# Attention outputs by blocks of keys, 512 queries wide, in two output and two transposition banks

## The chip, the cores and the metric

The kernel runs on one core of a Trainium2 chip. The core has TensorE (PE, with its weight loads as PEld), VectorE (DVE), ScalarE (ACT), GpSimd (POOL) and the queue engine SyncE (SP), each working through its own instructions in order. The metric is the device time of one execution in microseconds.

## The reference

One inference step of a two-layer decoder: a gated DeltaNet layer with its feed-forward network, one projection into shared keys and values, and a layer of sparse attention with its feed-forward network. It is done for a prompt of 512 positions and for 8 samples of 4 positions each. The part that matters is the attention of the prompt: 16 heads of 64, in 4 groups of key heads. Each query has three softmaxes, over compressed blocks, over the selected blocks and over a window, and the three results are added with gates:

```python
o_cmp = jnp.einsum('bkgqc,bckd->bqkgd', p_c, v_cmp)          # 31 compressed blocks
o_sel = jnp.einsum('bkgqsr,bkqsrd->bqkgd', p_s, v_g)         # selected blocks, key <= query
o_win = jnp.einsum('bkgqw,bwkd->bqkgd', p_w, v_win)          # window of 512, key <= query
o = jnp.stack([o_cmp, o_sel, o_win], axis=-1)
return jnp.einsum('bqhdr,bqhr->bqhd', o.astype(f32), gates)
```

With a prompt of 512, 16 selected blocks of 64 and a window of 512, the selected and the windowed keys of a query are all the keys up to its own position: for four blocks of 128 queries and four blocks of 128 keys, the ten pairs of blocks on and under the diagonal.

## The kernel before

The kernel keeps float32 accuracy by splitting a value into a high part (rounded to TensorE's fp32r, ScalarE, L158) and a low part (the rest, VectorE, L159); a product is then two or three products (high by high, low by high, high by low). Stages follow each other: DeltaNet, projections and a feed-forward network, the shared rows, the attention from 955 to 1222 us, and the last projection and feed-forward network.

In the attention stage (`attention`, L1453, with `self.banks(mm=4, aux=3, po=1)`, L1765) the 8 PSUM banks are named: four `mm` for scores and projections, three `aux` for transpositions, one `po` for a head's output. Each head has three steps, which run for different heads at a time:

- `prepare` (L1537) splits a head's queries into QH and QL.
- `scores` (L1553): for each of four blocks of 128 queries, products of QH and QL with the keys (L1566, L1567), bias and maximum on VectorE (L1449), the exponential on ScalarE (L1590), sums, and the scaling by gate over sum on GpSimd (L1604, L1606). The results lie in the tiles `uh` and `ul` as `P[r]`, one for each block r of queries.
- `outputs` (L1610) of the head before: the weights are transposed (L1641 for the compressed keys, L1656 for the other two types) into an `aux` bank, split into high and low tiles (CH and CL, or PT0 and PT1, two buffers of each), and multiplied with the values as the stationary operand (`VC`, `VT`: 64 columns of high parts, 64 of low parts). The products are added up in the `po` bank: L1621 and L1622 open it, L1629 adds to it. At the end one half of the bank's rows is copied (`otmp`, L1633) and added to the other half into `qf` (L1634).

`outputs` goes by two pairs of query blocks, 256 queries each. A pair has a unit of two transpositions for the compressed keys, and for each type units of two key blocks by two query blocks. The unit on the diagonal has only three transpositions; the missing block of both tiles is set to zero by GpSimd (L1651), and the products read it as if it were data. A head so has 24 transpositions in 8 units, and 28 products, all 256 wide. `flush` (L1662) writes the products of a unit into the program after the transpositions of the next one.

`weave` (L1501) mixes the steps of a head's scores, of the outputs of the head before and of the side work (`beside_heads`, L1506, by the table `SIDE`, L49: query projections, key and value pairs, the attention of the samples, and the last projection). The samples' attention fetches cached rows by gathers that GpSimd issues (L1333), and TensorE transposes those rows at L1354. The final order of each engine's instructions is set before the run by a scheduler (`schedule_with_timeline_sim`, L1803), which works from the order of the program, the dependences and the free buffers, and is then fixed.

Of the kernel before, what the change touches and what calls it, by code (L numbers as in the profile page):

```python
# [10 lines left out]
F32 = mybir.dt.float32  # L11
F32R = mybir.dt.float32r
# [3 lines left out]
OP = mybir.AluOpType  # L16
# [3 lines left out]
SEQ = 512  # L20
# [91 lines left out]
class Net:  # L112
# [206 lines left out]
    def deltanet(self, up, ctx):  # L319
# [560 lines left out]

        decays()
        run(plan(DN_START))
        for p, (text, inv, steps) in enumerate(DN_PAIRS):
            side = plan(text)
            self.weave([(zip(head(2 * p), head(2 * p + 1)), 4), (side, steps), (plan(inv), 6)])
            run(side)
        run(plan(DN_TAIL))
        return res

# [720 lines left out]
    def outputs(self, hd, sb):  # L1610


        T, V, S, G = self.T, self.V, self.S, self.G
        ident = self.C("ident")
        h, P = hd[0:2]
        g, q = h // 4, h % 2
        r0, r1 = slice(64 * q, 64 * q + 64), slice(64 - 64 * q, 128 - 64 * q)

        def first(th, tl):
            self.po = self.bank("po")[:, 0:256]  # L1620
            T.matmul(self.po, lhsT=self.VC[:, g], rhs=th, start=True, stop=False)  # L1621
            T.matmul(self.po, lhsT=self.VC[:, g], rhs=tl, start=False, stop=False)  # L1622

        def second(th, tl, pr, ty, k0):
            last = ty == 1 and k0 == 2 * pr
            for kb in (k0, k0 + 1):
                i = 2 * (k0 + 1 - kb)
                for m in (th, tl):
                    T.matmul(self.po, lhsT=self.VT[ty][:, kb, g], rhs=m[:, i:i + 2].rearrange("p e q -> p (e q)"),  # L1629
                             start=False, stop=last and kb > k0 and m is tl)  # L1630
            if last:
                tmp = sb.tile([128, 256], F32, name="otmp", bufs=1)
                S.copy(tmp[r0], self.po[r1])  # L1633
                V.tensor_tensor(self.qf[r0, h // 2, pr * 256:pr * 256 + 256], self.po[r0], tmp[r0], op=OP.add)  # L1634

        for pr in range(2):
            CH = sb.tile([128, 256], F32R, name="CH", bufs=1)
            CL = sb.tile([128, 256], F32R, name="CL", bufs=1)
            ps = self.aux()
            for e in range(2):  # L1640
                T.transpose(ps[:, e * 128:(e + 1) * 128], P[2 * pr + e][0][:, 0:128], ident)  # L1641
            self.split(CH, CL, ps[:, 0:256])
            self.flush(partial(first, CH, CL))
            for ty in range(2):
                for k0 in range(0, 2 * pr + 2, 2):

                    edge = k0 == 2 * pr
                    th, tl = [sb.tile([128, 4, 128], F32R, name=f"PT{x}") for x in range(2)]
                    if edge:
                        for t in (th, tl):  # L1650
                            G.memset(t.bitcast(F32)[:, 0], 0.0)  # L1651
                    ps = self.aux()
                    for i in range(edge, 4):
                        kb, e = k0 + 1 - i // 2, i % 2
                        a = (0 if ty else 32) + kb * 128
                        T.transpose(ps[:, i * 128:(i + 1) * 128], P[2 * pr + e][ty][:, a:a + 128], ident)  # L1656
                    b = slice(int(edge), 4)
                    self.split(th[:, b], tl[:, b], ps.rearrange("p (i q) -> p i q", q=128)[:, b])
                    self.flush(partial(second, th, tl, pr, ty, k0))
                    yield  # L1660

    def flush(self, nxt=None):  # L1662
        if self.pending:
# [68 lines left out]
    def run(self, ctx):  # L1732
        tc, A, O = self.tc, self.A, self.O
        up = ctx.enter_context(tc.tile_pool(name="up", bufs=8))
        self.nv = self.cst.tile([128, 41], F32, name="nv")
        self.nhalf = self.cst.tile([128, 17], F32, name="nhalf")
        self.G.memset(self.nhalf, -0.5)
        self.nvh = self.cst.tile([128, 1], F32, name="nvh")
        self.cw = self.cst.tile([128, 96], F32, name="cw")
        self.banks(mm=3, aux=2, ch=3)  # L1740
        with ExitStack() as c:
            og = self.deltanet(up, c)
        self.banks(mm=4, aux=4)
        self.page_rows()
        self.mid = ctx.enter_context(tc.tile_pool(name="mid", bufs=1))
        sblk = self.mid.tile([128, 4, NB, SCMP], F32, name="sblk")

        self.x = [None] * KD
        u2 = ctx.enter_context(tc.tile_pool(name="u2", bufs=8))
        with tc.tile_pool(name="xp", bufs=1) as xp:  # L1750
            self.load_x(xp)
            u, after = self.next_u(u2, 16)
            self.proj_add(A["dn_w_out"][0], 0, KD, og, after, done=[4 * (f"p{m}" in DN_PAIRS[3][0] + DN_TAIL) for m in range(KD)])
            rstd = self.rstd()
            ux, after = self.next_u(up, store=True)
            with tc.tile_pool(name="pb", bufs=2) as pb:
                self.ffn(0, u, rstd, after, self.beside(sblk, pb, up), 28)
            rstd = self.rstd()
        with tc.tile_pool(name="nsa", bufs=1) as np_:
            c2 = np_.tile([128, _CARR2.shape[1] - 2 * ESPAN], F32, name="c2")  # L1760
            self.dma(c2, A["const2"][:, 2 * ESPAN:])
            self.c2 = {k: c2[:, o - 2 * ESPAN:o - 2 * ESPAN + n] for k, (o, n) in _COFF2.items() if o >= 2 * ESPAN}
            tiles = [t.bitcast(F32) for _ in range(8) for t in self.u_tiles(u2)]
            self.shared(ux, rstd, np_, sblk, tiles)
            self.banks(mm=4, aux=3, po=1)  # L1765
            o = self.attention(ux, rstd, tiles, up, np_)
            self.banks(mm=4, aux=4)
        with tc.tile_pool(name="xp", bufs=1) as xp:
            self.load_x(xp, got=range(XM))
            u, after = self.next_u(u2, 24)  # L1770
            self.proj_add(A["nsa_w_out"][0], 0, KD, o, after, done=[XK] * XM + [0] * (KD - XM))
            rstd = self.rstd()
        with tc.tile_pool(name="yo", bufs=1) as yp:
            self.ffn(1, u, rstd, self.output(yp, up), self.window_rows(), 8)
# [32 lines left out]
```

## Time and profile before

| what | us |
|---|---|
| time, median of 3 runs | 1661.45 (1659.9 to 1662.36) |
| time of the profiled execution | 1664.61 |
| its span, first to last instruction | 1662.4 |
| TensorE busy in the span | 1596.2 (96%) |
| VectorE busy | 1059.6 (64%) |
| ScalarE busy | 710.8 (43%) |
| GpSimd busy | 562.3 (34%) |

The mean granted clock of TensorE is 0.985 of full speed. A busy share is that of the whole span; what a change in one stage is worth is read from that stage. In the chain of waits each piece is what the end of the work before it was waiting for, so the pieces of a stretch add up to it.

### The profile page before, as it was taken

What the parts mean: (1) busy time and instruction counts of PE and PEld (TensorE: products, weight loads), DVE (VectorE), ACT (ScalarE), POOL (GpSimd) and SP (SyncE); (2) the same over time, 40 slices, a digit from 0 to 9 for tenths busy, and PEclk for the clock granted to TensorE, in tenths of its full rate; (3) what the DMA queues carried; (4) which work ended last, traced back from release to release, by engine and by line L of the source; (5) the groups of instructions that cost most, each with busy time, mean ns of one, the idle gap of its engine ahead of it and who ended that gap; (6) DMA issues with size and microseconds to landing.
All of it is one profiled execution on the core that took longest, in us unless ns stands there. A gap on an engine that the chain in (4) does not pass through costs nothing.

```text
span 1662.4 us, 32746 instructions
## 1 busy us (share of the span) xinstructions
PE 1596.2 (96%) x12527; PEld 1526.5 (92%) x12527; DVE 1059.6 (64%) x2543; ACT 710.8 (43%) x1796; POOL 562.3 (34%) x861
## 2 busy tenths in 40 slices
PE   8998899998989999999999999999999999999997
PEld 6998788886989999999999899877999999999997
DVE  4878779477557753555456598677875553355533
ACT  5554554554322222233332488688843232132233
POOL 2776546424356621100045476565520000000000
PEclk9999999999999999999999999999999999999999
DMA  6233512256556635354343533523133332334232
GB/s 195 77 79 84 118 36 67 69 162 210 145 134 150 161 104 120 99 159 137 106 136 87 139 93 88 174 65 120 45 94 104 102 106 79 108 90 127 77 88 81
DMA packets 289068, 183.36 MB, mean 110 GB/s; under 512 B 25183, under 2 KB 271784, under 8 KB 288784
## 3 DMA queue, kind: packets, MB, share of 16 engines
q1 hardware_dynamic: 286352, 172.88, 38.0%
q0 software_dynamic: 2560, 8.39, 1.4%
q8 instruction: 98, 1.61, 0.4%
q14 instruction: 58, 0.48, 0.1%
HBM read 159.33 MB, written 26.90 MB: 112 GB/s over the span
## 4 chain that ended last, share of the span: by engine, by line
PE 76%; DVE 10%; POOL 4%; DMA 4%; ACT 3%; issue 3%; SPq 1%; POOLq 0%; DVEq 0%; ACTq 0%
PE mm L179 15%; PE mm L177 15%; PE mm L178 15%; PE aux L177 5%; PE aux L179 5%; PE aux L178 5%; PE po L1629 2%; PE aux L1656 2%; DVE hb L595 2%; DVE hb L597 1%; SPq L155 1%; DVE wlo L159 1%; PE mm L1566 1%; PE mm L818 1%; PE mm L1567 1%
## 5 line engine op out<-in xcount | busy, mean ns | idle before, releaser
L177 PE MATMUL mm<-uh,whi 128*128 128x288 f32 (+2 forms) x1824 | 531.5, 293 | 5.3 <-DVE hb L689 1.7
L178 PE MATMUL mm<-ul,whi 128*128 128x288 f32 (+2 forms) x1824 | 530.4, 292 | 0.0
L179 PE MATMUL mm<-uh,wlo 128*128 128x288 f32 (+2 forms) x1824 | 524.0, 292 | 4.8 <-DVE wlo L159 4.8
L158 ACT CAST whi<-wraw 128x1024 fp32r<-128x1024 f32 (+5 forms) x231 | 216.1, 936 | 525.6 <-PE mm L178 412.7
L177 PEld LDWEIGHTS mm<-uh,whi 128*128 128x128 f32 (+1 forms) x1824 | 344.2, 189 | 8.6 <-DVE hb L689 2.1
L179 PEld LDWEIGHTS mm<-uh,wlo 128*128 128x128 f32 (+1 forms) x1824 | 341.1, 189 | 6.9 <-DVE wlo L159 6.0
L178 PEld LDWEIGHTS mm<-ul,whi 128*128 128x128 f32 (+1 forms) x1824 | 344.6, 189 | 1.5 <-issue 0.4
L159 DVE TENSOR_TENSOR wlo<-wraw,whi 128x1024 fp32r<-128x1024 f32 (+5 forms) x207 | 233.1, 1126 | 108.6 <-ACT whi L158 107.1
L179 PE MATMUL aux<-uh,wlo 128*128 128x288 f32 (+1 forms) x704 | 202.1, 287 | 1.0 <-DVE wlo L159 0.9
L177 PE MATMUL aux<-uh,whi 128*128 128x288 f32 (+1 forms) x704 | 203.0, 288 | 0.0
L178 PE MATMUL aux<-ul,whi 128*128 128x288 f32 (+1 forms) x704 | 202.7, 288 | 0.0
L177 PE MATMUL mm<-hh,whi 128*128 128x256 f32 (+1 forms) x704 | 202.1, 289 | 0.0
L178 PE MATMUL mm<-hl,whi 128*128 128x256 f32 (+1 forms) x704 | 201.4, 288 | 0.0
L179 PE MATMUL mm<-hh,wlo 128*128 128x256 f32 (+1 forms) x704 | 196.5, 288 | 0.0
L184 POOL TENSOR_TENSOR ycol<-yvar,nhalf 128x2 f32<-128x2 f32 (+1 forms) x2 | 1.6, 776 | 398.0 <-DVE yvar L1704 398.0
L179 PEld LDWEIGHTS aux<-uh,wlo 128*128 128x128 f32 x704 | 132.4, 188 | 1.4 <-DVE wlo L159 1.4
L178 PEld LDWEIGHTS mm<-hl,whi 128*128 128x128 f32 x704 | 132.7, 188 | 0.0
L177 PEld LDWEIGHTS mm<-hh,whi 128*128 128x128 f32 x704 | 132.6, 188 | 0.0
L178 PEld LDWEIGHTS aux<-ul,whi 128*128 128x128 f32 x704 | 132.6, 188 | 0.0
L177 PEld LDWEIGHTS aux<-uh,whi 128*128 128x128 f32 x704 | 132.3, 188 | 0.2 <-issue 0.2
L179 PEld LDWEIGHTS mm<-hh,wlo 128*128 128x128 f32 x704 | 129.6, 188 | 0.0
L957 DVE SCALAR_TENSOR_TENSOR fup<-aux,rstd 128x256 f32<-128x256 f32 x88 | 38.7, 440 | 125.5 <-PE aux L179 125.5
(535 smaller groups left out, 2961.1 us busy)
## 6 DMA issues: line engine op xcount, KB each, us to landing
wraw<-in_ffn_w_in_dram SPq DMA_DIRECT2D x88, 512.0 KB
wraw<-in_dn_w_in_dram SPq DMA_DIRECT2D x32, 512.0 KB
wraw<-in_ffn_w_out_dram SPq DMA_DIRECT2D x32, 384.0 KB
wraw<-in_ffn_w_out_dram SPq DMA_DIRECT2D x32, 320.0 KB
hb<-in_state_dn_S_dram SPq DMA_DIRECT2D x32, 256.0 KB
wraw<-in_nsa_w_kv_dram SPq DMA_DIRECT2D x12, 512.0 KB
bskew<-bscr SPq DMA_DIRECT2D x16, 320.0 KB
x<-xd SPq DMA_DIRECT2D x16, 272.0 KB
```

Source lines behind the costliest of these rows:

```text
L155: return self.nc.sync.dma_start(out, in_)
L158: self.S.copy(hi, src)
L159: (self.G if pool_lo else self.V).tensor_tensor(lo, src, hi.bitcast(F32), op=OP.subtract)
L177: self.T.matmul(ps, lhsT=hi[:, k, :], rhs=uh[:, cs], start=first and k == 0, stop=False)
L178: self.T.matmul(ps, lhsT=hi[:, k, :], rhs=ul[:, cs], start=False, stop=False)
L179: self.T.matmul(ps, lhsT=lo[:, k, :], rhs=uh[:, cs], start=False, stop=last and k == kc - 1)
L595: V.tensor_tensor(t, D[a][:, 0:m, l:l + 1].to_broadcast([64, m, n]), row.to_broadcast([64, m, n]), op=OP.mult)
L597: V.tensor_tensor(N[a][:, 0:m, l:32], N[a][:, 0:m, l:32], t, op=OP.subtract)
L818: T.matmul(ps, lhsT=Kh, rhs=um[q], start=True, stop=True)
L957: V.scalar_tensor_tensor(up, pu, 0.5, rstd[:, cs], op0=OP.mult, op1=OP.mult)
L1629: T.matmul(self.po, lhsT=self.VT[ty][:, kb, g], rhs=m[:, i:i + 2].rearrange("p e q -> p (e q)"), start=False, stop=last and kb > k0 and m ...
L1656: T.transpose(ps[:, i * 128:(i + 1) * 128], P[2 * pr + e][ty][:, a:a + 128], ident)
```

## The change

`outputs` no longer goes by pairs of query blocks. One unit holds the compressed keys of all four query blocks (four transpositions, in the PT tiles, so CH and CL go). Then for each of the two types there are units of the key blocks 2 and 3 (three transpositions), 1 (three) and 0 (four), each with the query blocks from its own on. The products of key block kb are 512 - 128 kb wide and are added to that part of the one 512-wide `po` bank of the head. A head has 7 units, 24 transpositions, 18 products, one copy and one addition 512 wide, and no zeroing. The banks become `mm=4, aux=2, po=2`.

```diff
--- before.py
+++ after.py
@@ -1617,47 +1617,39 @@
         r0, r1 = slice(64 * q, 64 * q + 64), slice(64 - 64 * q, 128 - 64 * q)
 
         def first(th, tl):
-            self.po = self.bank("po")[:, 0:256]
+            self.po = self.bank("po")
             T.matmul(self.po, lhsT=self.VC[:, g], rhs=th, start=True, stop=False)
             T.matmul(self.po, lhsT=self.VC[:, g], rhs=tl, start=False, stop=False)
 
-        def second(th, tl, pr, ty, k0):
-            last = ty == 1 and k0 == 2 * pr
-            for kb in (k0, k0 + 1):
-                i = 2 * (k0 + 1 - kb)
+        def second(th, tl, ty, blocks):
+            for kb, o in blocks:
+                n = SEQ - 128 * kb
                 for m in (th, tl):
-                    T.matmul(self.po, lhsT=self.VT[ty][:, kb, g], rhs=m[:, i:i + 2].rearrange("p e q -> p (e q)"),
-                             start=False, stop=last and kb > k0 and m is tl)
-            if last:
-                tmp = sb.tile([128, 256], F32, name="otmp", bufs=1)
+                    T.matmul(self.po[:, 128 * kb:], lhsT=self.VT[ty][:, kb, g], rhs=m[:, o:o + n],
+                             start=False, stop=ty == 1 and kb == 0 and m is tl)
+            if ty == 1 and kb == 0:
+                tmp = sb.tile([128, SEQ], F32, name="otmp", bufs=1)
                 S.copy(tmp[r0], self.po[r1])
-                V.tensor_tensor(self.qf[r0, h // 2, pr * 256:pr * 256 + 256], self.po[r0], tmp[r0], op=OP.add)
-
-        for pr in range(2):
-            CH = sb.tile([128, 256], F32R, name="CH", bufs=1)
-            CL = sb.tile([128, 256], F32R, name="CL", bufs=1)
-            ps = self.aux()
-            for e in range(2):
-                T.transpose(ps[:, e * 128:(e + 1) * 128], P[2 * pr + e][0][:, 0:128], ident)
-            self.split(CH, CL, ps[:, 0:256])
-            self.flush(partial(first, CH, CL))
-            for ty in range(2):
-                for k0 in range(0, 2 * pr + 2, 2):
-
-                    edge = k0 == 2 * pr
-                    th, tl = [sb.tile([128, 4, 128], F32R, name=f"PT{x}") for x in range(2)]
-                    if edge:
-                        for t in (th, tl):
-                            G.memset(t.bitcast(F32)[:, 0], 0.0)
-                    ps = self.aux()
-                    for i in range(edge, 4):
-                        kb, e = k0 + 1 - i // 2, i % 2
-                        a = (0 if ty else 32) + kb * 128
-                        T.transpose(ps[:, i * 128:(i + 1) * 128], P[2 * pr + e][ty][:, a:a + 128], ident)
-                    b = slice(int(edge), 4)
-                    self.split(th[:, b], tl[:, b], ps.rearrange("p (i q) -> p i q", q=128)[:, b])
-                    self.flush(partial(second, th, tl, pr, ty, k0))
-                    yield
+                V.tensor_tensor(self.qf[r0, h // 2, 0:SEQ], self.po[r0], tmp[r0], op=OP.add)
+
+        def unit(srcs):
+            th, tl = [sb.tile([128, SEQ], F32R, name=f"PT{x}") for x in range(2)]
+            ps = self.aux()
+            for i, t in enumerate(srcs):
+                T.transpose(ps[:, i * 128:(i + 1) * 128], t, ident)
+            n = 128 * len(srcs)
+            self.split(th[:, 0:n], tl[:, 0:n], ps[:, 0:n])
+            return th, tl
+
+        self.flush(partial(first, *unit([P[r][0][:, 0:128] for r in range(4)])))
+        for ty in range(2):
+
+            for kbs in ((2, 3), (1,), (0,)):
+                cols = [(kb, r) for kb in kbs for r in range(kb, 4)]
+                a = 0 if ty else 32
+                th, tl = unit([P[r][ty][:, a + kb * 128:a + kb * 128 + 128] for kb, r in cols])
+                self.flush(partial(second, th, tl, ty, [(kb, 128 * cols.index((kb, kb))) for kb in kbs]))
+                yield
 
     def flush(self, nxt=None):
         if self.pending:
@@ -1762,7 +1754,7 @@
             self.c2 = {k: c2[:, o - 2 * ESPAN:o - 2 * ESPAN + n] for k, (o, n) in _COFF2.items() if o >= 2 * ESPAN}
             tiles = [t.bitcast(F32) for _ in range(8) for t in self.u_tiles(u2)]
             self.shared(ux, rstd, np_, sblk, tiles)
-            self.banks(mm=4, aux=3, po=1)
+            self.banks(mm=4, aux=2, po=2)
             o = self.attention(ux, rstd, tiles, up, np_)
             self.banks(mm=4, aux=4)
         with tc.tile_pool(name="xp", bufs=1) as xp:
```

The lines of the new kernel: L1621 and L1622 open the bank, L1628 adds to it, L1632 copies, L1633 adds into qf, L1639 transposes. TensorE has 11175 rows in its order where it had 11285, VectorE 2377 for 2409, ScalarE 1361 for 1388, GpSimd 673 for 801, SyncE 399 for 402.

In the middle of the stage, on TensorE, a unit of four blocks (into `aux`), a unit of three, and the products that open a bank (before; the number behind a name is that of its buffer):

```order
L1656 MATMUL aux<-ct,ul 128x128 x4
L179 MATMUL mm<-uh,wlo 128x288
L177 MATMUL mm<-uh,whi 128x288
L178 MATMUL mm<-ul,whi 128x288
L1656 MATMUL aux<-ct,ul 128x128 x3
L1621 MATMUL po<-CH,VC 128x256
L1622 MATMUL po<-CL,VC 128x256
L1629 MATMUL po<-PT_12309,VT_10325 128x256
L1629 MATMUL po<-PT_12310,VT_10325 128x256
L1629 MATMUL po<-PT_12309,VT_10325 128x256
```

The first product of the unit of four blocks stands 34 rows behind its transpositions:

```order
L1629 MATMUL po<-PT_12389,VT_10326 128x256
```

The like place in the new order, with two units transposed and multiplied (PT_11730 and PT_11731 are one unit, PT_11752 and PT_11753 that of the first transpositions shown):

```order
L1639 MATMUL aux<-ct,uh 128x128 x2
L1628 MATMUL po<-PT_11730,VT_10325 128x256
L1566 MATMUL mm<-x_10321,QH 128x416
L1567 MATMUL mm<-x_10321,QL 128x416
L1628 MATMUL po<-PT_11731,VT_10325 128x256
L1628 MATMUL po<-PT_11730,VT_10325 128x128
L1628 MATMUL po<-PT_11731,VT_10325 128x128
L1639 MATMUL aux<-ct,uh 128x128
L1639 MATMUL aux<-ct,ul 128x128
L1639 MATMUL aux<-ct,uh 128x128 x2
L1628 MATMUL po<-PT_11752,VT_10325 128x384
L1628 MATMUL po<-PT_11753,VT_10325 128x384
```

A unit's products now stand a few rows behind its transpositions, and the transpositions of the next unit between.

On GpSimd, the samples' gathers behind the scaling of a head, before:

```order
L1606 TENSOR_SCALAR uh<-uh,sums_13033,gt 128x512
L1606 TENSOR_SCALAR ul<-ul,sums_13033,gt 128x512
L1604 TENSOR_TENSOR uh<-uh,sg_13206 128x23
L1604 TENSOR_TENSOR uh<-uh,sg_13206 128x31
L1651 MEMSET PT_12993 128x128
L1651 MEMSET PT_12994 128x128
L1651 MEMSET PT_13043 128x128
L1651 MEMSET PT_13044 128x128
L1333 DMA ul<-in_cache_kv_dram,idx_sel 128x512
L1333 DMA uh<-in_cache_kv_dram,idx_sel 128x512
```

And after:

```order
L1604 TENSOR_TENSOR uh<-uh,sg_12915 128x7
L1333 DMA ul<-in_cache_kv_dram,idx_sel 128x512
L1606 TENSOR_SCALAR uh<-uh,sums_12871,gt 128x384
L1606 TENSOR_SCALAR ul<-ul,sums_12871,gt 128x384
L1606 TENSOR_SCALAR uh<-uh,sums_12871,gt 128x512
L1606 TENSOR_SCALAR ul<-ul,sums_12871,gt 128x512
L1604 TENSOR_TENSOR uh<-uh,sg_13022 128x23
L1604 TENSOR_TENSOR uh<-uh,sg_13022 128x31
L1333 DMA uh<-in_cache_kv_dram,idx_sel 128x512
```

The memsets between are gone, and one gather stands ahead of the scaling.

On TensorE at the end of the last head, before:

```order
L1656 MATMUL aux<-ct,ul 128x128 x3
L1621 MATMUL po<-CH,VC 128x256
L1622 MATMUL po<-CL,VC 128x256
L1629 MATMUL po<-PT_15434,VT_10325 128x256
L1629 MATMUL po<-PT_15435,VT_10325 128x256
L1629 MATMUL po<-PT_15434,VT_10325 128x256
L1629 MATMUL po<-PT_15435,VT_10325 128x256
L1629 MATMUL po<-PT_15446,VT_10325 128x256
L1629 MATMUL po<-PT_15447,VT_10325 128x256
L1629 MATMUL po<-PT_15446,VT_10325 128x256
L1629 MATMUL po<-PT_15447,VT_10325 128x256
L178 MATMUL mm<-ul,whi 128x288
```

And after:

```order
L1639 MATMUL aux<-ct,uh 128x128
L1639 MATMUL aux<-ct,ul 128x128
L1639 MATMUL aux<-ct,uh 128x128 x2
L1628 MATMUL po<-PT_15001,VT_10325 128x384
L1628 MATMUL po<-PT_15002,VT_10325 128x384
L1639 MATMUL aux<-ct,ul 128x128 x3
L1628 MATMUL po<-PT_15013,VT_10325 128x512
L1628 MATMUL po<-PT_15014,VT_10325 128x512
L1639 MATMUL aux<-ct,uh 128x128
L1639 MATMUL aux<-ct,ul 128x128 x2
L1628 MATMUL po<-PT_15024,VT_10326 128x256
L1628 MATMUL po<-PT_15025,VT_10326 128x256
```

The transpositions and products of the last units follow each other there with nothing between, where projection products stood between before.

## Rows read from the trace of the kernel before

**Rows 1.** Windows: from:to length, busy of PE PEld DVE ACT POOL, clock, DMA, GB/s.
```profile
955.00:1060.00 105.00, 104.85 (x821) 102.64 (x820) 90.01 (x313) 84.61 (x261) 68.78 (x146) 1.00 0.33 88
1060.00:1080.00 20.00, 16.48 (x113) 14.97 (x111) 10.83 (x41) 11.40 (x38) 15.17 (x27) 0.91 0.84 279
1080.00:1195.00 115.00, 111.75 (x867) 90.71 (x867) 94.93 (x402) 98.14 (x335) 64.55 (x160) 1.00 0.27 81
1195.00:1222.00 27.00, 26.09 (x216) 25.89 (x215) 16.60 (x34) 11.14 (x24) 6.40 (x18) 1.00 0.13 38
```

**Rows 2.** Chain of waits, 1052 to 1060: start us, us, what.
```profile
1054.12 0.17 PE mm L1567
...
1054.53 0.44 PE aux L1656 x4
...
1055.98 0.94 PE po L1629 x8
1056.91 0.24 PE mm L1566
```

**Rows 3.** Timeline, weight loads, at 334 and 938.
```profile
333.91 0.97 PEld L655 LDWEIGHTS aux<-hb 128*128 128x128 f32 x8 [0.86 <-issue]
...
937.62 0.74 PEld L1268 LDWEIGHTS aux<-ul,c 32*128 32x128 f32 x6
```

**Rows 4.** Lines by form, 950 to 1222: busy us, mean ns, idle before.
```profile
L158 ACT CAST PT<-aux 128x384 fp32r<-128x384 f32 x64 | 30.2, 475 | 6.6 <-PE po L1629 2.6 <-PE aux L1656 2.2 <-PE mm L1404 1.0
...
L1651 POOL MEMSET PT<- 128x128 f32 x124 | 22.1, 207 | 50.2 <-PE po L1629 45.5 <-DVE nm L1449 3.5 <-PE aux L1656 0.9
...
L158 ACT CAST PT<-aux 128x512 fp32r<-128x512 f32 x32 | 18.6, 583 | 14.1 <-PE po L1629 8.0 <-PE aux L1656 5.4
...
L1634 DVE TENSOR_TENSOR qf<-po,otmp 64x256 f32<-64x256 f32 x32 | 13.3, 417 | 3.4 <-ACT otmp L1633 2.8
...
L158 ACT CAST CH<-aux 128x256 fp32r<-128x256 f32 x32 | 11.8, 370 | 10.5 <-PE po L1621 8.2 <-PE aux L1641 1.1 <-PE aux L1656 0.9
...
L1633 ACT COPY otmp<-po 64x256 f32<-64x256 f32 x32 | 11.8, 368 | 3.8 <-PE po L1629 2.6 <-PE mm L1404 0.6
```

**Rows 5.** Waits, 1080 to 1195: engine, line, releaser, us in total, times, longest.
```profile
PEld po L1629 <- DVE PT L159: 2.5, 6, 0.8
...
PEld po L1621 <- DVE qf L1634: 0.8, 2, 0.6
PEld aux L1656 <- DVE PT L159: 0.8, 2, 0.4
```

**Rows 6.** Timeline, 1100 to 1106: start us, us, what.
```profile
1100.53 0.49 PE L1656 MATMUL aux<-ct,uh 128*128 128x128 f32 x3
...
1101.08 0.60 PE L1656 MATMUL aux<-ct,uh 128*128 128x128 f32 x4
1101.12 0.48 ACT L158 CAST PT<-aux 128x384 fp32r<-128x384 f32 x1
...
1101.74 0.56 DVE L159 TENSOR_TENSOR PT<-aux,PT 128x384 fp32r<-128x384 f32 x1
...
1105.00 0.69 DVE L159 TENSOR_TENSOR PT<-aux,PT 128x512 fp32r<-128x512 f32 x1 [0.35 <-ACT PT L158]
```

**Rows 7.** Chain of waits, 1061 to 1076.
```profile
1065.50 0.36 POOL ul L1333
...
1066.91 5.75 DMA uh<-in_cache_kv_dram,idx_sel
```

**Rows 8.** Windows, 1070 to 1078.
```profile
1070.00:1074.00 4.00, 1.34 (x10) 0.94 (x8) 2.27 (x10) 1.41 (x7) 3.08 (x4) 1.00 1.03 383
1074.00:1078.00 4.00, 3.60 (x14) 2.94 (x14) 0.28 (x1) 0.90 (x2) 2.50 (x6) 0.57 1.06 379
```

**Rows 9.** Chain of waits, the stage's end.
```profile
1217.77 0.94 PE po L1629 x8
...
1219.14 0.44 DVE qf L1634
```

## The prediction

> **What bounds the kernel now.** I read the windows first, then the chain of waits inside the attention stage, then its lines by form, its waits and single stretches of the timeline. The change touches only the attention stage, 955 to 1222 us, so only that stage is priced. In the windows TensorE is busy 104.85 of 105 us, 111.75 of 115 us and 26.09 of 27 us; ScalarE and VectorE, the busiest of the others, have 98.14 and 94.93 of the 115 us [rows 1]. Only 1060 to 1080 has a hole, 16.48 of 20 us. TensorE therefore sets the end of the stage, and a microsecond saved elsewhere counts only where TensorE waits for it. The chain says the same: its pieces are TensorE's own products, one behind the other [rows 2].
>
> **How long one TensorE instruction holds the engine.** In that chain eight 256-wide products take 0.94 us, 0.1175 each, and a 512-wide one 0.24, twice as much [rows 2]. A 384-wide one takes 0.17, and four transpositions 0.44, 0.11 each. So cost goes by columns, and one wide product is no cheaper than two halves. The Trainium skill (Perfetto Trace Analysis, Matmuls) says that larger matmuls are more efficient when possible; these rows show nothing of it between 256 and 512 columns, and by that rule the change would gain something more than the sum below.
>
> **1. Products: -4.5 us.** Before, a head has 28 products of 256 columns, 28 x 0.1175 = 3.29 us. After, it has 6 of 512, 4 of 384, 4 of 256 and 4 of 128 columns. I take 0.235, 0.17 and 0.1175 for the first three: 1.41 + 0.68 + 0.47 = 2.56 us. No product of the new kind with 128 columns stands in the trace. Halving the 256-wide gives 0.06. Six products 48 columns wide follow their weight loads, six loads in 0.74 us, 0.12 each, so narrow products seem held at 0.11 to 0.12 by the weights [rows 3]. Four fp32 products of 128 columns, each in two records, are eight loads in 0.97 us, which is 0.24 a product. I take 0.112, between half of the 256-wide and that row, as the transpositions, of the same width, have 0.11 [rows 2]: 0.45 us. The head then costs 3.01 us, 0.28 less, and 16 heads 4.5 us less. With 0.06 it would be 7.8 less, with 0.22 2.4 more. The number of transpositions stays 24 a head, 16 x 24 = 384.
>
> **2. Output bank: -1 us.** With one output bank the first product of a pair waits for the addition that drains it: twice, 0.8 us, in 1080 to 1195 [rows 5]. The second bank takes that away. It happens half as often as well, once a head.
>
> **3. Copies, sums and zeroing: 0.** ScalarE saves 0.31 us a head: before 2 x 0.370 + 4 x 0.475 + 2 x 0.583 for the splits and 2 x 0.368 for the copy [rows 4], 4.54 us; after 3 x 0.583 + 4 x 0.475, and 0.58 (estimate from the 512-wide) for one copy, 4.23 us. That is 5 us over 16 heads, VectorE's saving is of that size, and GpSimd loses its 124 memsets in the stage, 22.1 us busy and 50.2 us of standing before them [rows 4]. All of it lies beside TensorE's full engine. If that cover were gone it would show as shorter splits, which is counted in 5.
>
> **4. Gathers: -3 us.** GpSimd issues its cache gathers in its in-order queue at 1065.50 to 1066.91, behind the scaling of a head and four of the memsets; the transfer lands 5.75 us later [rows 7]. TensorE has run dry by then: 1.34 busy of 4 us from 1070, and then a clock of 0.57 of full speed for 4 us [rows 8]; of its two levels that is mostly the lower, 1.2 GHz. The hole of 1060 to 1080 is 20 - 16.48 = 3.5 us, and the clock costs 4 x 0.43 = 1.7, together 5.2 us. In the new order one gather stands before that scaling and the second directly behind it, with no memset between. I estimate the landing 1 us earlier, and more products stand on TensorE before the first that needs it: 3 us of the 5.2, with 0 and -5.2 as ends.
>
> **5. The distance from a unit's transpositions to its first product: +11.8 us.** This decides the sign. Behind a unit's last transposition ScalarE's cast and VectorE's subtraction must end before TensorE may use it. At best that takes from 1101.02 to 1102.30, 1.3 us; with a queue on these engines, from 1101.68 to 1105.69, 4.0 us [rows 6]. In the place shown of the old order 33 rows stand between a unit of four blocks and its first product; over all units it is 4 to 5 us of TensorE's work in the middle, adding these pitches along the order. In the new order the middle unit has 1.7 to 1.9 us to its high half. In the place shown the three instructions of the second unit's 384-wide product come after 0.12 + 2 x 0.19 + 0.12 + 2 x 0.11 + 4 x 0.11 = 1.28 us, less than the best latency. The reason is the third transposition bank that went: a bank is free only when its subtraction is done, so no unit can be transposed more than two ahead. TensorE is in order, so all projection products and scores queued behind such a product wait too, and ScalarE and VectorE after them. Before, in 115 us, six products wait for the split, 2.5 us in all, 0.42 each, and two transpositions wait for the bank, 0.8 us [rows 5]. That is six of some 55 units, one in nine. With less than half of the distance I take one in four of the 112 new units: 28 x 0.42 = 11.8 us. The ends are 0, if the queues on ScalarE and VectorE shrink as the TensorE order was planned, and 23.5, every second unit.
>
> The Trainium skill (Perfetto Trace Analysis, Optimization Strategy) says that the same gap repeated on the engine that should be saturated can mean too little PSUM for the next tile. The two transpositions that wait for a bank while three are there agree with it [rows 5]; no run here shows it with two.
>
> **6. The tail: +2 us.** The last head has nothing woven beside it. Its last eight products end at 1218.71 and the addition, 0.44 us, ends at 1219.58; the projection waits for it [rows 9]. Copy and sum are now 512 wide, some 0.21 and 0.27 us more (estimate, from 512 against 256 in the casts [rows 4], and the like for the sum). And the new order has transpositions and products of the last units back to back where eleven projection products stood between before: 0.67 to 1.14 us between a unit and its product where 1.3 is wanted, three or four times, 1.5 us. Ends 0 and 4.
>
> **The sum.** -4.5 - 1 + 0 - 3 + 11.8 + 2 = +5.3 us. The profiled execution took 1664.61 us (span 1662.4); with the change it would take 1669.9. It lies 3.16 us above the median of the runs, so from the median 1661.45 the sum gives 1666.7; I say 1666.
>
> **Rivals.**
> Short distances cost nothing new (faster). For it: the stage has fillers in plenty, and ScalarE's and VectorE's queues shorten with part 3, so that the 4.0 us latency may fall to near 1.3, under the new middle distance of 1.7 to 1.9. Against it: those two engines are busy 83 to 85% in 1080 to 1195 [rows 1], and waits are there even at 4 to 5 us. Term 5 is then 0, and the sum -6.5: 1655.
> Balance. The units wait as often as before, one in nine, less the older waits: 12 more waits at most, 5 us. The sum is -1.5: 1660.
> The 128-wide product holds TensorE for 0.22 (slower). For it: the fp32 products [rows 3]. Against it: the operands here are of the kind that runs in one record. It decides from about 0.19 on, where term 1 is above 0: 64 products x 0.108 = +6.9 us. With terms 2 to 6 that is 1673, and with a third of term 5 it is 1666.
> Two banks hold back the transpositions themselves, every second unit (slower). It is the far end of term 5: 16 to 17 us above the sum of the rest, -6.5 + 23.5 = +17: 1678.
> That the change does not do what it says can't be: the order has the widths, 6144 columns a head where 7168 were, and no memset.
>
> **How the numbers follow.** A run of this kernel tells 0.2%, 3.3 us, from no change. The forecast (short distances, with its far end) has 0.34, the wide price of the narrow product 0.09, balance 0.24, the faster rival 0.33. So slower 0.43, same 0.24, faster 0.33. The likeliest case's own range is 1665 to 1682. As both signs are likely, the range goes down to the faster rival and the lower narrow price, 1655 - 3.3, rounded to 1651, and up to 1682.
>
> **What would show it.** Term 1: the products' chain pieces, above all the 128-wide pitch. Term 2: no wait of a first product for the sum into qf. Term 4: TensorE's hole and its clock at the gathers. Term 5: in the waits of the stage, products waiting for the split and transpositions for the bank, of 10 us or more in all; the windows would have TensorE at some 93% of the stretch from 1080 on in place of 97%. Term 6: a gap before the first projection product of the next stage. I am wrong if these waits stay at some 3 us, or if the stage, 955 to the end of the sum into qf, is shorter than its 265 us.

## The result and the profile after

The changed kernel takes 1681.05 us (median of 4 runs, 1678.26 to 1683.47) against 1660.95 for the kernel before: a ratio of 1.0122 (95% interval 1.0106 to 1.0138), 20.1 us or 1.2% slower. The forecast was 1666 in a range of 1651 to 1682, with slower as the likeliest side. Its profiled execution took 1682.43 us, span 1680.6, at a mean clock of 0.984.

The windows of the new kernel, with the columns of [rows 1]; the stage now ends at 1236:

```profile
955.00:1060.00 105.00, 101.39 (x735) 94.48 (x734) 84.88 (x281) 76.81 (x231) 62.39 (x97) 1.00 0.31 82
1060.00:1080.00 20.00, 18.55 (x131) 16.30 (x129) 16.29 (x57) 15.46 (x49) 12.24 (x18) 1.00 0.63 203
1080.00:1195.00 115.00, 104.01 (x703) 75.56 (x704) 84.28 (x344) 86.42 (x285) 51.95 (x91) 0.97 0.30 90
1195.00:1236.00 41.00, 38.88 (x283) 35.37 (x282) 29.04 (x81) 23.88 (x64) 11.55 (x23) 1.00 0.17 50
```

TensorE is busy 104.01 us of the 115 from 1080 on, where it was 111.75 [rows 1]; that is 90% for 97. In the first 105 us it loses 3.6. VectorE, ScalarE and GpSimd too do less in this stretch, 84.28 us for 94.93, 86.42 for 98.14 and 51.95 for 64.55: no other engine has become the bound.

The waits of TensorE's weight loads in the stage, 945 to 1236 us (engine, line, releaser, us in total, times, longest):

```profile
PEld po L1628 <- DVE PT L159: 9.6, 20, 1.1
PEld po L1622 <- DVE PT L159: 2.5, 2, 1.5
...
PEld aux L1639 <- ACT ul L1190: 2.4, 2, 1.6
PEld po L1628 <- ACT PT L158: 2.2, 6, 1.1
...
PEld aux L1639 <- POOL uh L1604: 2.0, 1, 2.0
...
PEld mm L1566 <- DVE nm L1449: 1.8, 4, 0.8
...
PEld po L1621 <- ACT PT L158: 1.2, 3, 0.5
```

Products stand before the split of their unit in the four rows with `PT` behind the arrow, 9.6 + 2.5 + 2.2 + 1.2 us, 31 times, in 24 of the 112 units by the order of the instructions. Before, the list has one such row over the whole stage:

```profile
PEld po L1629 <- DVE PT L159: 3.0, 8, 0.8
```

How such a wait comes about, in the timeline at a place of the new order built like the one that the change's section shows:

```profile
1121.22 0.27 PE L1639 MATMUL aux<-ct,ul 128*128 128x128 f32 x1
...
1121.33 0.38 PE L1639 MATMUL aux<-ct,uh 128*128 128x128 f32 x2
...
1121.46 0.73 ACT L1590 ACTIVATE ul<-ul,nm 128x512 f32<-128x512 f32 x1
...
1122.08 0.38 PE L1639 MATMUL aux<-ct,uh 128*128 128x128 f32 x2
...
1122.18 0.31 ACT L1590 ACTIVATE uh<-uh,nm 128x31 f32<-128x31 f32 x1
...
1122.77 0.46 ACT L158 CAST PT<-aux 128x384 fp32r<-128x384 f32 x1
...
1123.28 0.55 DVE L159 TENSOR_TENSOR PT<-aux,PT 128x384 fp32r<-128x384 f32 x1
1123.28 0.44 PE L1628 MATMUL po<-PT,VT 128*128 128x384 f32 x1 [0.82 <-ACT PT L158]
...
1123.89 0.44 PE L1628 MATMUL po<-PT,VT 128*128 128x384 f32 x1 [0.17 <-DVE PT L159]
```

The unit's three transpositions (1121.22 and 1121.33) are done at 1121.71. Its cast stands behind exponentials of the scores on ScalarE, of which two are shown, and runs at 1122.77, the subtraction at 1123.28. TensorE meanwhile transposes the next unit, the last two blocks at 1122.08, which fills the second bank; then its queue holds the first unit's products, and it stands idle 0.82 us before the one and 0.17 before the other. From transposition to cast's end it took 1.5 us, and less work than that stood between.

The accounting of the stage, from the first score product to the last sum into `qf`, is by the starts of successive TensorE instructions in the trace. What an instruction took beyond the undisturbed spacing of its form is a wait, put to the instruction that then started. The length of the stage is read directly. The split into rows depends on the spacing taken as undisturbed: with the median between each two forms instead, single differences move by up to 3 us.

| us | before | changed | difference |
|---|---|---|---|
| stage | 275.3 | 289.9 | +14.6 |
| products into `po` | 52.9 | 46.8 | -6.1 |
| projections and scores | 129.7 | 129.7 | 0 |
| transpositions and fp32 products | 76.1 | 77.3 | +1.2 |
| waits of products into `po` | 5.4 | 13.0 | +7.6 |
| waits of the units' transpositions | 4.9 | 7.3 | +2.4 |
| waits of the cached rows' transpositions (L1354) | 3.6 | 5.7 | +2.1 |
| waits of scores | 1.8 | 4.7 | +2.9 |
| waits of projections | 1.3 | 2.5 | +1.2 |
| samples' products | -0.1 | 3.0 | +3.1 |

The stage explains 14.6 of the 18.2 us between the two spans. Behind it 2.2 us are lost, 442.9 to 445.1; ahead of it 1.5, which is no part of the change (the last section). The end of the stage in the chain of waits:

```profile
1229.21 0.59 ACT PT L158
1229.83 0.70 DVE PT L159
1230.57 0.50 PE po L1628
...
1232.31 0.60 ACT PT L158
1232.92 0.70 DVE PT L159
1233.67 0.52 PE po L1628
1234.21 0.59 ACT otmp L1632
1234.82 0.70 DVE qf L1633
1235.57 0.39 PE mm L177
...
1236.60 0.24 PE mm L177
1236.84 0.24 PE mm L178
```

Twice the chain leaves TensorE for a cast and a subtraction, then for the copy and the sum, now 0.59 and 0.70 us long. Before, the chain left it only for the copy and the sum [rows 9]. Behind it some of the projection products, which take 0.12 to 0.14 each at that place before, take 0.21 to 0.24. The windows show the clock there:

```profile
1080.00:1085.00 5.00, 3.58 (x18) 3.04 (x18) 3.04 (x10) 1.46 (x6) 3.72 (x5) 0.77 1.03 377
1085.00:1090.00 5.00, 3.68 (x36) 2.50 (x35) 1.54 (x8) 3.24 (x9) 1.34 (x5) 0.88 0.35 110
1150.00:1155.00 5.00, 3.19 (x18) 2.05 (x18) 4.88 (x22) 4.49 (x17) 2.07 (x6) 0.94 0.00 0
1155.00:1160.00 5.00, 5.00 (x32) 2.97 (x28) 0.41 (x1) 0.86 (x2) 3.37 (x6) 0.72 0.65 178
1235.00:1240.00 5.00, 4.43 (x23) 4.43 (x24) 1.21 (x2) 0.62 (x1) 0.00 (x0) 0.66 0.02 3
```

The granted clock falls below full speed three times, each time behind a hole in TensorE's work: the wait for the gathers (1.89 us), a row of waits at 1151 to 1154, and the tail. From 5 x (1 - clock) the three cost 1.75, 1.7 and 1.7 us, the last of them in the next stage. Before there was one such stretch, 1074 to 1078 [rows 8].

### The profile page after: what moved, and what is told of

It is laid out like the page before. It is cut to its first block, busy times and chain, and to the rows that moved or that the text cites. A ratio compares the mean times of both kernels' runs of the same rounds, so it can differ in the third digit from the quotient of the medians.

```text
span 1680.6 us, 32160 instructions
## 1 busy us (share of the span) xinstructions
PE 1600.4 (95%) x12367; PEld 1515.4 (90%) x12367; DVE 1063.2 (63%) x2511; ACT 706.4 (42%) x1764; POOL 540.5 (32%) x733
## 4 chain that ended last, share of the span: by engine, by line
PE 76%; DVE 10%; DMA 5%; POOL 3%; ACT 2%; issue 2%; SPq 1%; POOLq 0%; DVEq 0%; ACTq 0%
PE mm L177 15%; PE mm L179 15%; PE mm L178 15%; PE aux L177 5%; PE aux L179 5%; PE aux L178 5%; PE po L1628 2%; PE aux L1639 2%; DVE hb L595 2%; DVE hb L597 1%; DVE wlo L159 1%; PE mm L818 1%; PE mm L1566 1%; SPq L155 1%; PE mm L1567 1%
## 5 line engine op out<-in xcount | busy, mean ns | idle before, releaser
L159 DVE TENSOR_TENSOR wlo<-wraw,whi 128x1024 fp32r<-128x1024 f32 (+5 forms) x207 | 242.8, 1173 | 108.1 <-ACT whi L158 106.3
L179 PEld LDWEIGHTS mm<-hh,wlo 128*128 128x128 f32 x704 | 129.7, 188 | 0.0
```

The lines of the kernel that those rows point to most:

```text
L159: (self.G if pool_lo else self.V).tensor_tensor(lo, src, hi.bitcast(F32), op=OP.subtract)
L179: self.T.matmul(ps, lhsT=lo[:, k, :], rhs=uh[:, cs], start=False, stop=last and k == kc - 1)
```

## The experiments

Times are medians, beside before on the same chip; "stage" is that of the one profiled execution, as in the table above. That execution can lie off the median: e1's took 1664.45 us and e8's 1678.32. In the expectations, theory A says that the lost third transposition bank made the distances short, rival B that the new blocks themselves make the waits, and rival C that the new order is bad by chance at the gathers; rivals D and E are said where they come up.

| kernel | blocks | banks mm, aux, po | us | before | ratio (95%) | stage |
|---|---|---|---|---|---|---|
| e6_new_again | new | 4, 2, 2 | 1681.76 | 1664.90 | 1.0096 (1.0074 to 1.0118) | 290.0 |
| e2_old_2t2o | old | 4, 2, 2 | 1687.07 | 1663.38 | 1.0149 (1.0123 to 1.0176) | 297.0 |
| e5_old_2t1o | old | 4, 2, 1 | 1684.12 | 1664.90 | 1.0110 (1.0087 to 1.0133) | 294.0 |
| e4_new_lag2 | new | 4, 2, 2 | 1672.91 | 1663.38 | 1.0064 (1.0039 to 1.0089) | 279.3 |
| e3_new_mm3 | new | 3, 3, 2 | 1676.98 | 1663.38 | 1.0091 (1.0064 to 1.0119) | 288.1 |
| e1_new_3t1o | new | 4, 3, 1 | 1671.67 | 1663.38 | 1.0048 (1.0030 to 1.0066) | 274.9 |
| e12_new_3t1o_again | new | 4, 3, 1 | 1669.42 | 1665.53 | 1.0021 (1.0005 to 1.0036) | 278.4 |
| e7_new_3t1o_rev | new | 4, 3, 1 | 1676.18 | 1664.90 | 1.0060 (1.0038 to 1.0082) | 280.7 |
| e8_new_3t1o_lag2 | new | 4, 3, 1 | 1669.78 | 1664.90 | 1.0031 (1.0017 to 1.0045) | 282.7 |
| e11_new_3t1o_tail | new | 4, 3, 1 | 1673.14 | 1665.53 | 1.0042 (1.0025 to 1.0059) | 282.4 |
| e9_old_7shared | old | 7 shared, 1 | 1695.20 | 1665.53 | 1.0171 (1.0145 to 1.0198) | 293.7 |
| e10_new_7shared | new | 7 shared, 1 | 1716.61 | 1665.53 | 1.0298 (1.0271 to 1.0325) | 318.0 |

**The banks alone.** e2_old_2t2o is the kernel before with one line changed, e5_old_2t1o the same without the second output bank:

```diff
-            self.banks(mm=4, aux=3, po=1)
+            self.banks(mm=4, aux=2, po=2)   # e2
+            self.banks(mm=4, aux=2, po=1)   # e5
```

> The old pairs of query blocks with the new bank counts (mm=4, aux=2, po=2), nothing else. Theory A: slower than before by as much as the change lost in waits, 1675 to 1688 us, with 25 or more products waiting for the split. Rival B: as before, 1657 to 1664 us. Rival C: anything within some 8 us of before, with the number of products that wait for the split near the eight of before.

> The old pairs of query blocks with one transposition bank fewer and nothing in its place (mm=4, aux=2, po=1; seven banks). Theory A (the third transposition bank alone): 1680 to 1692 us, as with two and two. Rival D (what cost 24 us there was the pair of output banks, or the two together, through another order): within 6 us of before.

Both as theory A said. With the old blocks untouched, the third transposition bank is worth 19 to 24 us. Each count of banks also gives another order of instructions, so this is the worth of the bank together with the order made for it. The waits of the two, e2 first, then e5:

```profile
PEld po L1629 <- DVE PT L159: 7.9, 19, 1.1
PEld po L1629 <- ACT PT L158: 5.8, 9, 1.3
```

```profile
PEld po L1629 <- DVE PT L159: 7.9, 19, 1.0
PEld po L1621 <- DVE qf L1634: 4.2, 7, 1.7
```

Products wait for the split 28 times in e2 and some 21 in e5, against 8. The last row, seven waits for the sum into `qf`, is what the second output bank takes away; it stands in e5 and not in e2, and e2 is no faster for it. The Trainium skill (Perfetto Trace Analysis, Matmuls) asks that independent groups rotate through different PSUM banks, so that draining one overlaps the products of the next; here the wait for the drained bank went, and the time did not.

**The new blocks with the old banks**, twice:

```diff
-            self.banks(mm=4, aux=2, po=2)
+            self.banks(mm=4, aux=3, po=1)
```

> The new blocks of keys, but with the bank counts of before: three transposition banks, one output bank (mm=4, aux=3, po=1). Theory A (the lost third transposition bank made the distances short): the waits for the split go back to some 3 us and the narrower products stay won, so 1652 to 1661 us, with waits of a first product for the sum into qf (one output bank) of at most 5 us in it. Rival B (the new blocks themselves make the waits: units of unequal size, wide copy and sum): little changes, 1674 to 1683 us. Rival C (the new order is bad by chance at the gathers): the time follows TensorE's hole at the gathers, and products wait as often as in the changed kernel.

> The new blocks with three and one banks once more, for a second profile. Its runs lay in two groups, near 1664 and near 1672, and the profile was of the first. If the groups come from ahead of the stage, where the order of instructions is that of before: a stage of 273 to 277 us again. If from the stage: in a run near 1672 a stage of 280 us or more.

Theory A's direction holds, its number does not: 8 to 17 us better than the changed kernel by the ratios to before, with a stage 11 to 15 us shorter, but 4 to 8 us above before, where it had said equal or faster. From the waits of e1:

```profile
PEld po L1628 <- DVE PT L159: 4.7, 8, 1.4
...
PEld mm L177 <- DVE qf L1633: 1.8, 1, 1.8
PEld po L1628 <- ACT PT L158: 1.7, 4, 1.0
PEld po L1622 <- DVE PT L159: 1.7, 2, 1.2
...
PEld mm L1354 <- DVE qf L1633: 1.1, 1, 1.1
PEld po L1621 <- DVE qf L1633: 1.1, 1, 1.1
```

The products into `po` are again 46.8 us, 6.1 less than before, and the waits of the stage 23.1 and 26.3 in the two profiles, against 16.8. So what the columns save is spent on waits in the stage, some of it on products of units (9.0 and 9.6 against 5.4). The wide sum stands behind one opening product, 1.1 us, and by the list behind one transposition of cached rows, besides the tail. Within the stage the two profiles come out about even with before, 0.4 us shorter and 3.1 longer; behind it they lose another 3.2 and 4.5 us (446.1 and 447.4 for 442.9), 1.7 and some 3 of it at a lower clock. The two groups of e1's runs were not found again in e12, and the second stage, 278.4 us, lies between the two expected; that question stays open.

**The distance at two banks.** e4_new_lag2 puts a unit's products two units behind:

```diff
+        self.queue.append(nxt)
+        if nxt is None or len(self.queue) > 2:
+            ...
-            th, tl = [sb.tile([128, SEQ], F32R, name=f"PT{x}") for x in range(2)]
+            th, tl = [sb.tile([128, SEQ], F32R, name=f"PT{x}", bufs=3) for x in range(2)]
-                tmp = sb.tile([128, SEQ], F32, name="otmp", bufs=1)
+                tmp = P[3][1][:, 0:SEQ]
```

> The changed kernel (mm=4, aux=2, po=2), with a unit's products written two units behind its transpositions in place of one, three buffers of each PT tile, and the copy of the output in a tile of the head's weights that is no longer read (this makes room). Theory A in its narrower form (it is the distance on TensorE alone that counts, whatever the banks): the middle distance to the low half grows from 2.6 to 3.2 us, so a good part comes back, 1665 to 1675 us. If the transpositions' waiting for a bank is what counts and not the distance: no change, 1677 to 1684. Rival B: no change either.

As theory A's narrower form said: 5 to 10 us better than the changed kernel by the ratios to before, with a stage 10.6 us shorter, with the same two banks. The step also gives each PT tile a third buffer, and the two are not told apart here. Its waits:

```profile
PEld aux L1639 <- DVE PT L159: 3.5, 7, 0.8
...
PEld po L1628 <- ACT PT L158: 2.4, 4, 1.3
...
PEld po L1621 <- ACT PT L158: 1.4, 2, 0.9
...
PEld po L1628 <- DVE PT L159: 0.5, 1, 0.5
```

The products' waits for the split fall to 7 and 4.3 us in the list, where the changed kernel has 31 and 15.5, and before 8 and 3.0. What stays are the waits of the units' transpositions, in the accounting 9.5 us for 7.3. Seven of them, 3.5 us, now stand behind the subtraction that frees a bank; the changed kernel has none behind a subtraction and 2.4 us behind a copy that frees one (`ul`, L1190, in its list). So with two banks a longer distance moves part of the wait from the products to the transpositions.

**Three and two banks, the scores paying.** e3_new_mm3 (`mm=3, aux=3, po=2`):

> The new blocks with three transposition banks and two output banks, the eighth bank taken from the scores and projections (mm=3, aux=3, po=2). Theory A: 1653 to 1665 us, better than the changed kernel by 15 us or more, unless three banks for scores put new waits in front of the score products; then 1665 to 1675 with those waits in the list. Rival B: 1675 to 1690 us.

Missed for theory A: 1676.98 us is above the 1675 of its worse case, and inside rival B's range (which e2 and e5 exclude as the cause of the main loss). Product waits fall to 8.0 us, but the projections wait 5.1 us (2.5) and the cached rows' transpositions 8.9 (5.7). The scores themselves wait no longer than in the changed kernel. The stage is only 1.8 us shorter than its 289.9, so what the third transposition bank gave was lost again at these other waits; that the bank taken from the projections causes them was not tested by itself.

**Other orders with three and one banks.** e7 runs the key blocks 0, 1, (2, 3); e8 is the delayed form of e4; e11 moves two steps of the last projection:

```diff
-            for kbs in ((2, 3), (1,), (0,)):
+            for kbs in ((0,), (1,), (2, 3)):        # e7
-  "sosssoosossos", "sooso", "", "os")
+  "sosssoosossos", "sso", "", "ooos")              # e11
```

> The new blocks with three transposition banks and one output bank, key blocks 0, 1, then 2 and 3, so that the last products of a head are narrow. Theory A: the distances are as in the first such kernel (5.0 us in the middle to the low half), so 1660 to 1670 us. Rival E (with three and one banks it is the wide copy and sum before the next head's first product that costs): no better than 1668 to 1675, with waits of the opening products for the sum into qf of 5 us or more.

> The new blocks with three transposition banks and one output bank, and products two units behind their transpositions with three buffers of each PT tile. Theory A in its narrower form (distance): the distance is already long with three banks (4.85 against 4.73 us in the middle to the low half), so the step adds little: 1660 to 1672 us. If the waits left with three banks came from the two PT buffers: 1655 to 1662.

> The new blocks with three and one banks, and two steps of the last projection moved from the head before the last to the end (a line of the table SIDE), so that the last units have projection products between them again. If the bare end of the stage costs the 2 us of waits and the lower clock behind it: 3 us better than e1_new_3t1o, 1664 to 1669 us. If the wait for the last sum into qf alone counts: no change.

e7 missed theory A's range, without rival E's waits either: its opening products wait for the sum into `qf` 1.0 us in all. But its products wait for their split 15 times, 12.2 us by the list, not far below the 15.5 of the changed kernel, though it has three transposition banks and by its order distances as long as e1's. A long distance in the middle is then not enough. e8 is inside the range; its products wait 4.7 us, its transpositions 6.5, its scores 6.8. e11 shows no gain. All four orders of the new blocks with three and one banks lie 4 to 11 us above before, and none of these three steps is measurably better than e1 and e12.

**Distance without banks of their own.** e9 and e10 let scores, projections and transpositions take turns at seven banks (the lines for e9; e10 has the same, from `mm=4, aux=2, po=2`):

```diff
+        tag = tag if tag in self.nb else "mm"
-            self.banks(mm=4, aux=3, po=1)
+            self.banks(mm=7, po=1)
```

> The old pairs of query blocks, with the seven banks for scores, projections and transpositions shared by all three in turn, and one output bank. In the order the middle distance to the low half grows from 5.0 to 7.1 us and the changes from transposition to product fall from 75 to 56. Theory A (distance): product waits of before, 4.9 us in the stage, nearly go; 1655 to 1662 us here, where before has 1660 to 1666. If before is already long enough and scores now wait for their banks: 1663 to 1672.

> The new blocks with the seven shared banks and one output bank. Middle distance 4.3 us, but 19 units under 2.5 us where the new blocks with three and one banks have 10; 67 changes from transposition to product for 77. Theory A: near the new blocks with three and one banks, 1664 to 1672 us. If the number of banks in the transpositions' reach counted and not the distance: better than those by 5 us, 1658 to 1664.

Both far off, against theory A in its bare form. e9 has the longest distance of all kernels, and is 30 us slower than before, 18.4 of it in the stage; e10's product waits are 27.7 us, twice the changed kernel's. In the waits of e9 and of e10 (lines stand one lower in the file: L1642 and L1640 transpose):

```profile
PEld mm L1642 <- POOL uh L1605: 5.1, 6, 1.7
```

```profile
PEld po L1629 <- DVE PT L160: 15.5, 27, 1.4
PEld mm L1640 <- POOL uh L1607: 15.2, 13, 3.0
PEld po L1629 <- ACT PT L159: 9.6, 14, 1.5
```

Transpositions now stand before weights that GpSimd has yet to scale. In e10 that is a large part of the loss; in e9 it is 5.1 us, and the rest of the 18.4 is spread over many rows and was not traced further. A distance that is long in the planned order is no saving when what stands ahead of the transposition is late itself.

**The changed kernel again.**

> The changed kernel once more, timed beside the same runs of before as the other kernels here. All theories: 1676 to 1686 us. Its instructions up to 937 us stand in the same order as those of before, so if the start of the stage moves between executions by several us, as between the other profiles (940 to 949 us), the stage itself, from the first score product to the last sum into qf, should stay at 287 to 292 us.

As expected: stage 290.0 us for 289.9, with each class of waits within 0.7 us of the table.

## Why the prediction was right, and where its size was not

The side and the mechanism held: slower, by products that wait for their split behind two transposition banks. That the bank is the cause e2 and e5 show, and e4 that the distance has a part in it. The size was 5 us where 20 came. The range held by 1 us at its upper end, and it was 31 us wide because both signs had been thought likely (slower 0.43), so that it held says little. The rival at 1678 came nearer in time, but not as it was put: 24 of 112 units wait, not every second.

- Products: -4.5 was taken, -6.1 came. A pair of 128-wide products takes 0.17 us, 0.060 from the first to the second and 0.110 from that to its successor, 0.085 each: between the lower end and the value taken. The rival of 0.22 falls.
- Output bank: -1. The wait for the sum did go, 1.1 us in the stage before and none after. But opening products wait 3.7 us for the split instead (2.5 + 1.2 in the waits above, which count with the short distances), so nothing was gained there, as e2 beside e5 shows too.
- Copies and zeroing, 0: right; both engines are idler and nothing came of it.
- Gathers: -3 is the step that failed outright. "The second directly behind it, with no memset between" came true, and it is that second one which TensorE waits for, as three rows of the new kernel show, the end of the scaling and the issue on GpSimd, and the first transposition of the gathered rows on TensorE; below them the like wait of before, from its list:

```profile
1073.83 1.01 POOL L1604 TENSOR_TENSOR uh<-uh,sg 128x23 f32<-128x23 f32 x2
1075.01 1.04 POOL L1333 DMA_INDIRECT uh<-in_cache_kv_dram,idx_sel  x1 [0.16 <-issue]
...
1081.42 0.33 PE L1354 MATMUL mm<-ct,uh 128*128 128x128 f32 x1 [1.89 <-DMA uh<-in_cache_kv_dram,idx_sel]
```

```profile
PE mm L1354 <- issue: 2.1, 1, 2.1
```

  The early gather helped nothing. The second is issued 129.3 us after the stage's first score product, where it was 122.7 (1066.91 [rows 7] less 944.2), 6.6 us later. TensorE had stood idle 4.4 us of the stage by then, 0.3 before, so that most of the delay is likely that of the scores and the scaling ahead of it; no run shows this by itself. The hole stayed, 1.89 us for 2.1, and so did its price in clock, 1.75 for 1.7: the term came out near 0. The +2.1 in the accounting comes from two later waits of transposed cached rows, at 1133.6 and 1135.0 us, so that the row as a whole is 5 us off.
- Short distances: +11.8, from 28 waits of 0.42 us. Measured are 31 waits of 0.50, 15.5 us of the weight loads' time, 3.0 of it there before. The forecast counted units, of which 24 wait, so the count was nearly right. What the term left out is what it named, the work queued behind, by the accounting: scores +2.9 us, transpositions +2.4, samples' products +3.1, some of it at the lower clock.
- Tail: +2 was taken. By the waits from 1225 on it is 3.2 against 1.07, +2.1. The lower clock behind it, 1.7 us, was not in the sum.

In the stage, then, the terms compare like this. Products -6.1 for -4.5; the cached rows' transpositions +2.1 for the -3 of the gathers; the output bank, the short distances and the tail together +12.8 in the forecast, and +18.6 by the accounting (what is left of the 14.6). That is 14.6 for 5.3. Behind the stage come 2.2 us, and 1.5 between executions ahead of it. From profile to profile the execution grew by 17.8 us, and between the medians by 20.1.

The Trainium skill's rule on repeated gaps and too little PSUM (Perfetto Trace Analysis, Optimization Strategy), which no run could speak on before, is borne out by e2 and e5: with two transposition banks for three, products wait for the split 28 and 21 times for 8.

That the new blocks gain nothing with the old banks is measured, and that in the stage their saved columns reappear as waits is in the accounting. Why this order waits more, with nearly the distances of before (4.7 for 5.0 us in the middle), is not settled: the wide sum shows too few waits for it, and neither another order of key blocks nor a further delay removes it.

## What to carry to other kernels

Where one in-order engine sets the end, a buffer that lets another engine run ahead can be worth more than a few per cent of that engine's work: here 19 to 24 us against the 6.1 of the narrower products. Count, from the new order, how much work stands between a unit's first step and its use, and set it against the latency with queues, not the best one. A short distance is a warning; a long one is no promise (e7, e9). Price a wait with what stands behind it and with the clock that falls after it. And when a change bundles a saving with a new split of buffers, run the split alone first.

## What the runs showed that was not expected

Up to 916 us the instructions of the changed kernel, e1 to e4 and before stand in the same order on every engine. Still, the first score product starts at 944.2, 945.7, 941.7, 948.5, 940.5 and 948.2 us in their profiles (before, changed, e1 to e4), 8 us apart, and nearly all of it arises between 416 and 560 us. Differences of a few us between single profiles are therefore read from the stage and not from the span.

A stretch at a lowered clock cost 1.7 us or near it in most profiles: 1.75, 1.7 and 1.7 in the changed kernel, 1.7 in before. But e3 and e8 each have one of some 3.4 us behind the gathers, and e6 one of 5.1 from 1150 on. In e10, with the most waits, it is 15.3 us in all between 930 and 1290. These sums are of the granted clock in windows of 5 us, as above.
